# Decoder block on one core: token rows stored from ScalarE's queue, one gather ahead of a looped conditional part, and expert rows stored at once and added by eight adding gathers

## The chip, the cores and the metric

The kernel runs on one core of one Trainium2 chip. A core has a matrix engine (TensorE, here PE, with its weight loads as PEld), a vector engine (VectorE, DVE), an engine for activations and scaled copies (ScalarE, ACT), a general engine (GpSimd, POOL) and one that mostly issues transfers (SyncE, SP). Each engine runs its own instructions in their order; they wait for each other by semaphores. The metric is the device time of one execution in microseconds (us).

## The reference

One layer of a hybrid decoder, for 512 tokens of 1024 features in float32. The first half (a gated DeltaNet beside a gated MLP over the sequence) is untouched here. Its sum with the input is normalized per token; the result `h` goes into a mixture of 16 experts, and the sum of `h` and the experts' rows is normalized again:

```python
h = layer_norm(DEEPNORM_ALPHA * h + mix, ln1_g[l], ln1_b[l])
# routing: the best of 4 groups, in it the best 2 of 4 experts, with their weights
h_e = silu(t @ expert_w_gate[e]) * (t @ expert_w_up[e])      # 1024 -> 256
y  += combine[:, e] * (h_e @ expert_w_down[e])               # 256 -> 1024
h = layer_norm(DEEPNORM_ALPHA * h + ffn, ln2_g[l], ln2_b[l])
```

Every token goes to two experts.

## The kernel before

The 512 tokens are NT=4 tiles of 128 rows; `HT[:, i]` holds the rows of tile i (128 partitions by 1024 features). An instruction list in strings (L1015 to L1017) writes out the order of the first norm and the routing: `c`, `e` are parts of the last product of the first half, `t` transposes, `l` router logits, `f` is `finish(i)` (the norm of tile i), `g` is `choose(i)` (group and experts), `r` is `ranks(i)` (a token's place in its expert's list), and `w8` makes PE do eight products of no use.

`finish(i)` splits a row between engines: DVE does the first w columns (L965, L974), ACT and POOL the others (L971 to L973), with w=384, and 1024 for the last tile. It then stores the tile's rows in DRAM (`hD`, L975, from SP's queue).

`rank_tokens` (L1043) makes `idx`: for each expert a list of at most CAP=128 tokens. `gather(e)` (L1064) is a DMA that POOL issues: it fetches the rows of expert e's tokens from `hD` into one of five buffers `XG[e % 5]`. Two of them, gather(0) and gather(1), are issued ahead of a conditional part (L1100), which treats experts with more than 128 tokens in further blocks of 128; it is written out per block inside a loop over the experts. With these inputs no expert has as many, and every engine jumps over it, after it has read the largest count (L1097).

Weights come in 8 KB buffers (16 of them, per partition): `eload` (L800) loads a third of an expert (half of gate and up, or all of down), `esplit` (L818) splits it into a high part (ACT, L829) and a low part (DVE, L833), since each float32 product is done as three products of such parts (`kmm3`). A buffer that PE has used goes back to the ring and takes the next load (`release`, L1213); some are kept out of it.

For each expert `turn(e, hh)` (L1198) transposes its gathered rows on PE (L1205) and splits them on ACT (L1207) and DVE (L1208), `gate_up(e, part)` (L1226) does the first products in two halves, `swiglu` the gate, `down(e, n)` (L1242) the second product. `down` scales the result on ACT (L1261) into `yo[e]`. The experts are pipelined: in the loop's round e PE does `gate_up(e + 1)`, `turn(e + 2)` and `down(e)`.

What becomes of `yo[e]`: for e < E0=3 it is a gather buffer and is stored at once in DRAM (`yD`). For e = 3 to 11 (NL=12) it stays in SBUF, in buffers kept out of the ring of loads, and is stored after the last load of weights (L1359). Two rows of `yD` per token are then fetched by eight plain gathers (L1371) into `YG`, and added to `HT`: five adds by POOL (L1376), two by DVE at L1333, one by DVE at L1423. The rows of the last four experts are not stored: products with one-hot matrices (`rows_of_last`, L1272, PE L1278) place them. `total(i)` (L1384, DVE L1388) adds those to `HT`, and `inv_std`, `half1` (L1403) and `half2` do the second norm.

`K(...)` marks instructions that a scheduler leaves in the written order. The others, gathers among them, it may place elsewhere, as long as `tc.issue_after` and the data allow it.

## Time and profile before

| | us |
|---|---|
| time before, median of 3 runs | 812.68 (812.58 to 812.73) |
| profiled execution, its own time | 813.55 |
| its span in the trace | 811.8 |
| PE idle in 616.2 to 623.2 | 7.0 |
| one expert, from 641.4 to 650.8 on | 9.40 |
| last gather of `yD` rows issued | 776.5 |
| PE's last product ends | 792.2 |

The span is what the trace shows from the first to the last instruction; the execution's own time is 1.75 us more. A line of a timeline has the start, the time that a group took, the engine, the line of the code, and what it reads and writes. A number in square brackets is how long the engine had been idle, with what ended it.

### The profile page before, as it was taken

To read this page: it belongs to the slowest core of one execution; us is meant where nothing else is said; L and a number is where in the kernel's file an instruction comes from. 1 tells how busy PE (TensorE), PEld (TensorE's weight loads), DVE (VectorE), ACT (ScalarE), POOL (GpSimd) and SP (SyncE) were. 2 spreads that over 40 slices of the span, in tenths; PEclk is the share of its full clock that TensorE was granted. 3 is DMA by queue.
4 is the path that set the end of the run, shared out by engine and by line. 5 is a ranking of instruction groups with operands and counts; after the bars stand their busy time and mean duration, and the time that the engine had idled before them with its cause. 6 is when DMAs were issued, how large, how long until landed. Compare 5 with 4: busy or idle time off the path is not lost. (4 is left out here: it accounts for less than half of the span.)

```text
span 811.8 us, 10918 instructions
## 1 busy us (share of the span) xinstructions
PE 772.2 (95%) x4043; PEld 642.1 (79%) x4043; DVE 536.0 (66%) x1011; ACT 383.6 (47%) x646; POOL 114.7 (14%) x104
## 2 busy tenths in 40 slices
PE   8999999999999999999999999999985999999990
PEld 7688888887899988888888888888764788888780
DVE  3558954997567954357542322334598999999987
ACT  2545763553334624324222222222325999999833
POOL 2030002000100000002410101000132112100276
PEclk9999999999999999999999999999996999999996
DMA  9970045447230155234274323399628999999752
GB/s 232 225 210 16 1 74 135 80 99 150 52 89 2 29 128 103 63 95 104 44 200 122 92 84 91 100 326 343 212 96 274 345 381 382 368 346 289 275 227 103
DMA packets 105936, 133.65 MB, mean 165 GB/s; under 512 B 18628, under 2 KB 87672, under 8 KB 105880
## 3 DMA queue, kind: packets, MB, share of 16 engines
q1 hardware_dynamic: 101528, 118.08, 49.6%
q0 software_dynamic: 4352, 14.84, 5.4%
q8 instruction: 33, 0.54, 0.3%
q14 instruction: 23, 0.19, 0.1%
HBM read 120.82 MB, written 12.08 MB: 164 GB/s over the span
## 5 line engine op out<-in xcount | busy, mean ns | idle before, releaser
L239 PE MATMUL pa<-r,r 128*128 128x512 f32 (+1 forms) x688 | 268.8, 391 | 0.0
L240 PE MATMUL pa<-r,r 128*128 128x512 f32 (+1 forms) x688 | 268.2, 390 | 0.1
L241 PE MATMUL pa<-r,r 128*128 128x512 f32 (+1 forms) x688 | 267.8, 389 | 0.0
L150 DVE TENSOR_TENSOR r<-r,r 128x2048 fp32r<-128x2048 f32 (+2 forms) x57 | 103.6, 1821 | 126.5 <-ACT r L149 125.7
L149 ACT ACTIVATE r<-r 128x2048 fp32r<-128x2048 f32 (+2 forms) x57 | 86.7, 1528 | 137.3 <-PE pa L240 81.6
L239 PEld LDWEIGHTS pa<-r,r 128*128 128x128 f32 x688 | 129.4, 188 | 26.2 <-issue 0.9
L241 PEld LDWEIGHTS pa<-r,r 128*128 128x128 f32 x688 | 129.3, 188 | 25.7 <-DVE r L713 0.2
L240 PEld LDWEIGHTS pa<-r,r 128*128 128x128 f32 x688 | 129.3, 188 | 25.6 <-DVE r L745 0.5
L833 DVE TENSOR_TENSOR r<-r,r 128x1024 fp32r<-128x1024 f32 x96 | 117.1, 1222 | 4.7 <-ACT r L829 3.0
L829 ACT ACTIVATE r<-r 128x1024 fp32r<-128x1024 f32 x96 | 96.3, 1059 | 0.0
L1227 PE MATMUL pa<-r,r 128*128 128x512 f32 x192 | 78.1, 407 | 0.0
L1229 PE MATMUL pa<-r,r 128*128 128x512 f32 x192 | 75.9, 395 | 1.0 <-DVE r L1329 1.0
L1228 PE MATMUL pa<-r,r 128*128 128x512 f32 x192 | 75.6, 394 | 0.0
L398 DVE SCALAR_TENSOR_TENSOR r<-pa,r,r 128x509 f32<-128x509 f32 (+2 forms) x72 | 53.4, 746 | 9.9 <-ACT r L396 9.1
L1229 PEld LDWEIGHTS pa<-r,r 128*128 128x128 f32 x192 | 36.0, 188 | 9.8 <-DVE r L1329 1.9
L1228 PEld LDWEIGHTS pa<-r,r 128*128 128x128 f32 x192 | 36.3, 189 | 7.0
L1227 PEld LDWEIGHTS pa<-r,r 128*128 128x128 f32 x192 | 36.2, 189 | 7.1 <-ACT r L1207 0.2
L1066 POOL DMA_INDIRECT r<-hD,r x16 | 20.2, 1263 | 90.9 <-PE pb L1205 38.6
L399 ACT ACTIVATE r<-r 128x512 f32<-128x512 f32 x24 | 15.0, 627 | 31.9 <-DVE r L398 26.5
L782 POOL TENSOR_TENSOR r<-r,r 128x512 f32<-128x512 f32 x8 | 10.3, 1291 | 137.4 <-DVE r L781 133.2
L743 POOL TENSOR_TENSOR r<-r,r 128x512 f32<-128x512 f32 x8 | 14.2, 1787 | 98.0 <-DVE r L740 94.8
L396 ACT ACTIVATE r<-pa,r 128x512 f32<-128x512 f32 x24 | 16.3, 684 | 24.3 <-PE pa L241 24.3
(335 smaller groups left out, 934.5 us busy)
## 6 DMA issues: line engine op xcount, KB each, us to landing
r<-in_w_in_dram SPq DMA_DIRECT2D x22, 1024.0 KB, 8.4
r<-in_expert_w_gate_dram SPq DMA_DIRECT2D x32, 512.0 KB, 7.7
r<-in_expert_w_down_dram SPq DMA_DIRECT2D x16, 1024.0 KB, 8.9
r<-in_expert_w_up_dram SPq DMA_DIRECT2D x32, 512.0 KB, 8.1
r<-in_w_in_dram SPq DMA_DIRECT2D x20, 512.0 KB, 10.5
yD<-r SPq DMA_DIRECT2D x12, 512.0 KB, 9.7
r<-in_x_dram SPq DMA_DIRECT2D x8, 512.0 KB, 7.3
r<-in_w_dn_out_dram SPq DMA_DIRECT2D x4, 1024.0 KB, 5.2
```

Source lines behind the costliest of these rows:

```text
L149: pin(A.activation(hi, raw, AF.Copy))
L150: pin(eng.tensor_tensor(lo, raw, f_(hi), ALU.subtract))
L239: pin(T.matmul(o, lh, rh, start=first, stop=False))
L240: pin(T.matmul(o, lh, rl, start=False, stop=False))
L241: pin(T.matmul(o, ll, rh, start=False, stop=last))
L398: V.scalar_tensor_tensor(acc[:, s:], p[:, :S - s], wc(3 - s), acc[:, s:], op0=ALU.mult, op1=ALU.add)
L829: K(A.activation(hi[:, s], raw[:, s], AF.Copy))
L833: K(V.tensor_tensor(lo[:, s], raw[:, s], f_(hi[:, s]), ALU.subtract))
L1066: return G.indirect_dma_start(out=XG[e % 5], out_offset=None, in_=hD, in_offset=bass.IndirectOffsetOnAxis(ap=idx[:, e:e + 1], axis=0))
L1227: K(T.matmul(args[0], args[1], args[3], start=args[5], stop=False))
L1228: K(T.matmul(args[0], args[1], args[4], start=False, stop=False))
L1229: K(T.matmul(args[0], args[2], args[3], start=False, stop=args[6]))
```

## The change

Four things, in the order of the code.

1. `finish`: w=384 only for tiles 0 and 1, so tile 2 is DVE's alone, too. The store of the rows to `hD` is issued by ACT. The last `eload` is no longer held until the last such store. `w10` stands for `w8`, and 16 more products of no use follow the list.
2. Only gather(0) is issued ahead of the conditional part. Expert 0's first turns, a weight split and the first half of its products come ahead of it, too. Gathers 1 to 4 follow a fence (`gbehind`) behind it. The conditional part itself is now two loops, over blocks and over experts and blocks.
3. Every expert's rows, e < 12, are stored at once into `yD`, from ACT's queue, and `yo[e]` is always a gather buffer. Only one load buffer is kept out of the ring. gather(e + 5) is issued in round e.
4. In round 11, eight gathers with `compute_op=ALU.add` fetch rows of `yD` and add them to `HT[:, i]`. The plain gathers and the adds on POOL and DVE are gone.

```diff
     def finish(i):
-        w = 384 if i < NT - 1 else D
+        w = 384 if i < NT - 2 else D
...
-        stored[i] = SP.dma_start(hD[i * 128:(i + 1) * 128], HT[:, i])
+        A.dma_start(hD[i * 128:(i + 1) * 128], HT[:, i])
...
-                   t33 l33 f3 g3 w8 r3""".split():
+                   t33 l33 f3 g3 w10 r3""".split():
...
     eload()
-    with tc.issue_after(stored[NT - 1].ins):
-        eload()
+    eload()
...
     rank_tokens(idx, RO)
+    warm(16)
...
     earlier = esplit(0, True)
-    gather(0)
-    second = gather(1)
+    first = gather(0)
...
+    earlier()
+    turn(0, 0)
+    turn(0, 1)
+    esplit(1)
+    gate_up(0, 0)
...
-    with tc.issue_after(second.ins):
+    with tc.issue_after(first.ins):
         most = nc.values_load(cmi[0:1, 0:1], min_val=0, max_val=S,
...
-        for b in range(1, NBLK):
-            V.tensor_scalar(ork, rk2, float(CAP * b), None, op0=ALU.subtract)
+        V.tensor_copy(ork, rk2)
+        with tc.For_i(0, NBLK - 1, 1) as bo:
+            V.tensor_scalar(ork, ork, float(CAP), None, op0=ALU.subtract)
...
-            for b in range(1, NBLK):
-                SP.dma_start(oi, iD[bass.ds(eo * (NBLK - 1) + (b - 1), 1)].rearrange("b p o -> p (b o)"))
+            with tc.For_i(0, NBLK - 1, 1) as bo:
+                SP.dma_start(oi, iD[bass.ds(bo * NE + eo, 1)].rearrange("b p o -> p (b o)"))
...
+    gbehind = G.memset(gto[:, 1, 0:1], 0.0)
...
-    gather(2)
+    with tc.issue_after(gbehind.ins):
+        gather(1)
+        gather(2)
...
-    later()
-    turn(0, 0)
-    turn(0, 1)
     splits()
-    gate_up(0, 0)
-    gather(3)
-    gather(4)
+    gate_up(0, 1)
+    with tc.issue_after(gbehind.ins):
+        gather(3)
+        gather(4)
...
     def store(e):
-        SP.dma_start(yD[e * CAP:(e + 1) * CAP], yo[e])
+        K(A.dma_start(yD[e * CAP:(e + 1) * CAP], yo[e]))
...
-            yo[e] = reg(kept.popleft(), D) if e >= E0 else XG[(e + 2) % 5]
+            yo[e] = XG[(e + 2) % 5]
         K(A.activation(yo[e][:, ns], p, AF.Copy, scale=w_))
-        if n == 1 and e < E0:
+        if n == 1:
             store(e)
...
-        if E0 <= e < NL and (e == E0 or not (e - E0) % 2 == 0):
+        if e == E0:
             owed[0] += 1
...
-            for n in range(2):
-                K(V.tensor_tensor(HT[:, 0], HT[:, 0], YG[0][n], ALU.add))
...
-        if e <= E0:
-            gather(e + 5)
-        if e == E0:
-            gather(e + 6)
-        if e >= E0:
-            gather(e + 7)
+        gather(e + 5)
...
-        if e == NL:
-            with tc.issue_after(last_load[0].ins):
-                for m in range(E0, NL):
-                    store(m)
-        if e == NE - 3:
-            YG = [yo[m] for m in range(E0, NL)] + [reg(kept_rk, D)]
...
-            for i in range(NT):
-                for n in range(2):
-                    K(G.indirect_dma_start(out=YG[i][n], out_offset=None, in_=yD,
-                                           in_offset=bass.IndirectOffsetOnAxis(ap=sli[:, i, n:n + 1], axis=0)))
-            for i in range(1, NT):
-                for n in range(2):
-                    if i + n > 1:
-                        K(G.tensor_tensor(HT[:, i], HT[:, i], YG[i][n], ALU.add))
+        if e == NL - 1:
+            for n in range(2):
+                for i in range(NT):
+                    K(G.indirect_dma_start(out=HT[:, i], out_offset=None, in_=yD,
+                                           in_offset=bass.IndirectOffsetOnAxis(ap=sli[:, i, n:n + 1], axis=0),
+                                           compute_op=ALU.add))
...
-    K(V.tensor_tensor(HT[:, 1], HT[:, 1], YG[1][0], ALU.add))
```

What the change moves is seen in the order of each engine's instructions: line, operation, written<-read, shape, and the semaphores that it waits for (DMAHW and DMASW are those of transfers). The first piece is ACT at the start of the routing, as a difference; r_3260 is `HT`, L971 is in `finish`, L949 in `logits_part`, L938 in `transposes`.

```order
 L938 ACTIVATE r_4336<-pb 128x256 [waits PE_49,Activation_49]
 L971 ACTIVATE r_3260<-r_3260,r_3002,r_3000 128x640 [waits DVE_49]
+L975 DMA hD<-r_3260 128x1024 [waits DVE_49,DMAHW1_49,Activation_49,Pool_49]
 L949 ACTIVATE r_4312<-pa 20x128 [waits PE_49]
 L962 ACTIVATE r_4333<-r_2998,r_4331 128x1 [waits DVE_49]
-L938 ACTIVATE r_4337<-pb 128x256 [waits PE_49,Activation_49]
-L938 ACTIVATE r_4338<-pb 128x256 [waits PE_49,Activation_49]
+L938 ACTIVATE r_4337<-pb 128x256 [waits PE_49]
+L938 ACTIVATE r_4338<-pb 128x256 [waits PE_49]
 L971 ACTIVATE r_3260<-r_3260,r_3002,r_3000 128x640 [waits DVE_49]
-L949 ACTIVATE r_4312<-pa 20x128 [waits PE_49,Activation_49]
```

The store of a tile's rows now stands on ACT behind its L971, waiting for POOL and DVE, and ahead of the next L949.

The second place is POOL at the conditional part. Before, from the last step of `finish` on (r_4771 and r_4772 are the buffers of gathers 0 and 1):

```order
L973 TENSOR_TENSOR r_3260<-r_3260,r_4101 128x640 [waits Pool_49]
L1066 DMA r_4771<-hD,r_4741 128x1024 [waits DMAHW2_49,DMAHW4_49,DMAHW1_49,DMAHW7_49,DVE_49,Pool_49]
L1066 DMA r_4772<-hD,r_4741 128x1024
L1097 TENSOR_LOAD r_4769 [waits DVE_49]
L1100 COMPARE_AND_BRANCH
```

Both gathers stand ahead of the branch. At the end of the conditional part before (r_4773 is gather 2's buffer, the next into r_4771 is gather 5):

```order
L1100 UNCONDITIONAL_BRANCH
L1100 ISA [waits DMASW4_49,DMASW5_49,DMASW3_49,DMASW6_49,DMASW2_49,DMASW7_49,DMASW1_49,DMASW0_49]
L1100 UNCONDITIONAL_BRANCH
L1066 DMA r_4773<-hD,r_4741 128x1024 [waits DMASW4_49,DMASW5_49,DMASW3_49,DMASW6_49,DMASW2_49,DMASW7_49,DMASW1_49,DMAHW1_49,DMASW0_49,DMAHW4_49,DVE_49,DMAHW5_49,PE_49,Activation_49]
L1066 DMA r_4771<-hD,r_4741 128x1024 [waits PE_49]
```

The ISA row waits for all gathers issued so far. After, from the last step of `finish` on (r_4787 is expert 0's buffer; the second DMA into it is gather 5):

```order
L973 TENSOR_TENSOR r_3260<-r_3260,r_4101 128x640 [waits Pool_49]
L1066 DMA r_4787<-hD,r_4740 128x1024 [waits DMAHW2_49,DMAHW3_49,DMAHW1_49,DMAHW7_49,DVE_49,Pool_49]
L1066 DMA r_4787<-hD,r_4740 128x1024 [waits DMASW6_49,PE_49]
L1198 TENSOR_LOAD r_4785 [waits DVE_49]
L1201 COMPARE_AND_BRANCH
```

In gather 1's place stands gather 5. At the end of the conditional part after (r_4788 to r_4790 are the buffers of gathers 1 to 3):

```order
L1201 UNCONDITIONAL_BRANCH
L1201 ISA [waits DMASW4_49,DMASW5_49,DMASW3_49,DMASW6_49,DMASW2_49,DMASW7_49,DMASW1_49,DMASW0_49]
L1201 UNCONDITIONAL_BRANCH
L1263 MEMSET r_4871 128x1 [waits DVE_49]
L1066 DMA r_4788<-hD,r_4740 128x1024 [waits DMASW1_49]
L1066 DMA r_4789<-hD,r_4740 128x1024 [waits DMASW4_49,DMASW3_49,DMASW5_49,DMASW2_49,DMASW6_49,DMASW0_49,DMASW7_49,DVE_49,DMAHW1_49,PE_49,Activation_49]
L1066 DMA r_4790<-hD,r_4740 128x1024 [waits PE_49,Activation_49]
```

Gather 1 has moved from ahead of the branch to behind the fence (the MEMSET), and gather 5 from behind the conditional part to ahead of it, where it waits for a step of PE.

The third place is ACT in the round of expert 4. Before (r_5649 is the kept buffer of `yo[4]`):

```order
L1267 ACTIVATE r_5074<-pa 128x256 [waits DVE_49]
L829 ACTIVATE r_5637<-r_5301 128x1024 [waits DMAHW3_49]
L829 ACTIVATE r_5637<-r_5301 128x1024
L1261 ACTIVATE r_5649<-pa,r_4742 128x512 [waits PE_49] x2
L829 ACTIVATE r_5680<-r_5319 128x1024 [waits DMAHW5_49,DMAHW6_49,DVE_49,Activation_49]
L829 ACTIVATE r_5680<-r_5319 128x1024
```

Nothing stands between `down`'s steps and the next split copies. After (r_4788 is a gather buffer):

```order
L829 ACTIVATE r_5539<-r_5201 128x1024 [waits DMAHW3_49]
L829 ACTIVATE r_5539<-r_5201 128x1024
L1168 ACTIVATE r_4788<-pa,r_4741 128x512 [waits DMASW5_49,DMASW1_49,PE_49]
L1168 ACTIVATE r_4788<-pa,r_4741 128x512 [waits PE_49]
L1102 DMA yD<-r_4788 128x1024 [waits DMAHW3_49,Activation_49]
L829 ACTIVATE r_5581<-r_5219 128x1024 [waits DMAHW6_49,DVE_49]
L829 ACTIVATE r_5581<-r_5219 128x1024
```

The store of `yD` now follows the two steps of `down` on ACT, with a wait for a transfer's semaphore of its own, and the next split copies (L829) stand behind it.

## Rows read from the trace of the kernel before

**Rows 1.** The page of the profile: the span, and the line of each engine's busy time, its share of the span and its instructions.
```profile
span 811.8 us, 10918 instructions
...
PE 772.2 (95%) x4043; PEld 642.1 (79%) x4043; DVE 536.0 (66%) x1011; ACT 383.6 (47%) x646; POOL 114.7 (14%) x104
```

**Rows 2.** The table of stretches: from and to in us, length; then busy time and (in brackets) instructions of each engine, the clock granted to TensorE as a share of full speed, the DMA engines' mean busy share, and GB/s.
```profile
616.20:623.20 7.00, 0.00 (x0) 0.00 (x0) 5.55 (x25) 3.80 (x6) 2.08 (x2) 0.51 0.95 320
...
623.20:632.00 8.80, 8.76 (x45) 7.08 (x46) 7.78 (x18) 5.58 (x7) 4.28 (x4) 0.81 0.72 224
...
641.40:650.80 9.40, 9.40 (x48) 7.78 (x47) 9.30 (x11) 8.22 (x13) 0.00 (x0) 1.00 1.07 381
...
792.20:811.80 19.60, 0.00 (x0) 0.00 (x0) 14.12 (x34) 6.50 (x13) 12.31 (x10) 0.63 0.28 107
```

**Rows 3.** The timeline of VectorE in the routing: start us, us, engine, line, operation, out<-in, shape.
```profile
602.05 0.62 DVE L974 SCALAR_TENSOR_TENSOR r<-r,r,r 128x384 f32<-128x384 f32 x1
...
603.21 1.63 DVE L985 TENSOR_TENSOR r<-r 128x80 f32<-128x80 f32 x1
...
604.87 1.57 DVE L986 TENSOR_TENSOR r<-r,r 128x80 f32<-128x80 f32 x1
...
611.32 1.28 DVE L974 SCALAR_TENSOR_TENSOR r<-r,r,r 128x1024 f32<-128x1024 f32 x1
...
613.12 0.24 DVE L985 TENSOR_TENSOR r<-r 128x80 f32<-128x80 f32 x1
...
616.16 0.17 DVE L1050 CAST r<-pb 128x16 int32<-128x16 f32 x1
```

**Rows 4.** Around the first rows' store: a line of POOL's timeline, one of ACT's, and the instructions of line 975 on SyncE's queue in 612 to 613 us (durations ns min/median/max).
```profile
586.61 1.54 POOL L973 TENSOR_TENSOR r<-r,r 128x640 f32<-128x640 f32 x1
...
587.16 0.27 ACT L949 ACTIVATE r<-pa 20x128 f32<-20x128 f32 x1 [2.33 <-PE pa L947]
...
L975 SPq DMA_DIRECT2D hD<-r x1: 338/338/338, 612.6 to 612.6; - x1
```

**Rows 5.** POOL's timeline at the first gathers, and from the view of line 1066 how long a gather took from issue to landing, first for the one issued at 617.2, then for the one at 626.8.
```profile
617.15 1.11 POOL L1066 DMA_INDIRECT r<-hD,r  x1 [10.81 <-DVE r L1085]
...
626.81 0.94 POOL L1066 DMA_INDIRECT r<-hD,r  x1 [7.27 <-DVE r L1208]
...
DMA to landing us min/median/max: 5.9/5.9/5.9
...
DMA to landing us min/median/max: 4.7/4.7/4.7
```

**Rows 6.** PE's timeline from the pause on; in square brackets the idle time before a group and what ended it.
```profile
623.25 1.94 PE L1205 MATMUL pb<-r,r 128*128 128x128 f32 x8 [7.12 <-DVE r L1181]
...
625.02 0.79 PE L1227 MATMUL pa<-r,r 128*128 128x512 f32 x1
...
632.00 0.60 PE L1205 MATMUL pb<-r,r 128*128 128x128 f32 x4
...
632.46 0.48 PE L1227 MATMUL pa<-r,r 128*128 128x512 f32 x1
...
640.70 0.50 PE L1229 MATMUL pa<-r,r 128*128 128x512 f32 x1 [0.62 <-DVE r L1329]
```

**Rows 7.** The instructions of line 1100, the conditional part (q behind an engine's name is its sequencer): durations ns min/median/max, first and last start us.
```profile
L1100 PEldq COMPARE_BRANCH  x1: 5229/5229/5229, 616.7 to 616.7; - x1
...
L1100 DVEq COMPARE_BRANCH  x1: 76/76/76, 619.0 to 619.0; - x1
...
L1100 POOLq INC_SWDGE_SEM  x1: 512/512/512, 625.0 to 625.0; - x1
```

**Rows 8.** ACT's timeline in the twelfth and thirteenth expert.
```profile
746.48 1.27 ACT L1261 ACTIVATE r<-pa,r 128x512 f32<-128x512 f32 x2
...
753.22 0.60 ACT L1207 ACTIVATE r<-pb 128x512 fp32r<-128x512 f32 x1 [0.71 <-PE pb L1205]
```

**Rows 9.** The DMA view of 645 to 655 us (the mean rate, and the issues of the up weights: KB each, median us to landing), and the same issues in 685 to 695 us.
```profile
DMA packets 2632, 3.78 MB, mean 378 GB/s; under 512 B 98, under 2 KB 2247, under 8 KB 2632
...
r<-in_expert_w_up_dram SPq DMA_DIRECT2D x2, 512.0 KB, 8.1
...
r<-in_expert_w_up_dram SPq DMA_DIRECT2D x2, 512.0 KB, 10.8
```

**Rows 10.** The end of the kernel: line 1371's gathers and their landings, then lines of the timelines of POOL, DVE and PE.
```profile
L1371 POOL DMA_INDIRECT r<-yD,r x8: 937/956/1761, 765.4 to 776.5; - x8
...
DMA to landing us min/median/max: 5.3/10.1/10.6
...
781.44 13.86 POOL L1376 TENSOR_TENSOR r<-r,r 128x1024 f32<-128x1024 f32 x5 [4.04 <-DMA r<-yD,r]
...
777.40 2.47 DVE L1333 TENSOR_TENSOR r<-r,r 128x1024 f32<-128x1024 f32 x2
...
782.22 0.69 DVE L1388 SCALAR_TENSOR_TENSOR r<-pb,r 128x512 f32<-128x512 f32 x1 [0.36 <-PE pb L1278]
...
783.88 3.42 DVE L1423 TENSOR_TENSOR r<-r,r 128x1024 f32<-128x1024 f32 x1
...
799.92 0.68 DVE L1388 SCALAR_TENSOR_TENSOR r<-pa,r 128x512 f32<-128x512 f32 x1
...
790.18 1.98 PE L1278 MATMUL pb<-r,r 128*128 128x512 f32 x8
```

More of the change, by code (lines that the diff above doesn't have):

```diff
@@ L1189, in body @@
     FHL = carve(mixer_only, (2, 128), F32R)[0]
+    ZROW = NL * CAP
     yD = dram.tile([ZROW + 1, D], F32, name="yD")
@@ L1279, in rows_of_last @@
                            start=m == 0 and y is Y_LAST[m][0], stop=m == NE - NL - 1 and y is Y_LAST[m][1]))
+    earlier()
[3 more added lines that the diff above has]
+    gate_up(0, 0)
+    yO = dram.tile([(NBLK - 1) * NE * CAP, D], F32, name="yO")
+    iD = dram.tile([(NBLK - 1) * NE, CAP, 1], I32, name="iD")
+    with tc.issue_after(first.ins):
+        most = nc.values_load(cmi[0:1, 0:1], min_val=0, max_val=S,
+                              skip_runtime_bounds_check_because="a count of tokens")
@@ new lines, in body @@
+    A.activation(gto[:, 0, 0:1], ones[:, 0:1], AF.Silu)
+    SGB = cst(FF)
+    behind = V.memset(gto[:, 0, 1:2], 0.0)
+    gbehind = G.memset(gto[:, 1, 0:1], 0.0)
+    with tc.issue_after(behind.ins):
+        K(V.memset(SGB[0:4], 0.0))
+        GE, GB = cst(NT, 2, 16), cst(NT, 2, 3, 16, dt=BF16)
+        V.tensor_tensor(GE, EO, gt[:, :, :, None].to_broadcast([128, NT, 2, 16]), ALU.mult)
+        for n in range(3):
+            V.tensor_copy(GB[:, :, :, n], GE)
+            if n < 2:
+                V.tensor_tensor(GE, GE, GB[:, :, :, n], ALU.subtract)
+        slf, ovr = cst(NT, 2), cst(NT, 2)
+        V.tensor_scalar(ovr, rk2, float(CAP), None, op0=ALU.is_ge)
+        V.scalar_tensor_tensor(slf, eid, float(CAP), rk2, op0=ALU.mult, op1=ALU.add)
+        V.scalar_tensor_tensor(slf, ovr, float(ZROW), slf, op0=ALU.mult, op1=ALU.add)
+        V.tensor_scalar(sli, slf, float(ZROW), None, op0=ALU.min)
+        rs4 = cst(NT, NE - NL, 2)
+        V.tensor_tensor(rs4.rearrange("p i e n -> p i n e"), EO[:, :, :, NL:NE],
+                        rk2[:, :, :, None].to_broadcast([128, NT, 2, NE - NL]), ALU.mult)
+        V.tensor_reduce(rkv, rs4, axis=AX.X, op=ALU.add)
+        V.scalar_tensor_tensor(rkv, EA[:, :, NL:NE], -1.0, rkv, op0=ALU.add, op1=ALU.add)
@@ L1305, in body @@
     splits()
-    gate_up(0, 1)
     turn(1, 1)
```

151 lines of the change are left out of this document (59 added, 92 removed).

## Prediction

> **What bounds the kernel now.** I read the page's head first [rows 1]: TensorE (PE) is busy 772.2 of 811.8 us, so the question is where the other 39.6 lie. The table of stretches says it for this part of the kernel [rows 2]. From 616.2 to 623.2 PE does nothing: routing is done, the rows of expert 0 are being fetched. From 641.4 on each expert takes 9.40 us, all of them PE's; VectorE (DVE) has 9.30 of them and ScalarE (ACT) 8.22, and the DMA engines stand at a share of 1.07 with 381 GB/s. From 792.2 to the end PE is idle and DVE and GpSimd (POOL) finish the rows. So three stretches matter: the pause, the experts (bound by PE, with DVE and the DMA almost as full), and the tail. The timelines of each engine and the landings of the gathers give the waits inside them [rows 3 to 10].
>
> **Routing, up to the conditional part.** Two steps of the DVE chain, L985 and L986, take 1.63 and 1.57 us beside POOL's two steps of `finish(2)`, and 0.24 us each with POOL at rest [rows 3]. With i=2 all on DVE, POOL's part is gone: −1.63−1.57+2×0.24 = −2.7 us. DVE gets 1024 columns instead of 384 in its two steps; the row of i=3 has 1.28 for one against 0.62 for 384 columns: +1.3 us. Against it stands the stores' new queue. ACT is in order, and the store of rows 0 waits for POOL's last step, which ends at 586.61+1.54 = 588.15; L949, which ran at 587.16, stands behind it (the order's first place) and would start some 1.3 us later, with the 0.34 us of issuing that SP's store shows [rows 4]. PE had other work there, so I charge 0.5 of these 1.3; the same at `finish(1)` costs about as little. The cast of the list of indices goes ahead of another, −0.2. Sum −0.7 with 0.2 for the second store's wait; ends −1.6 (the stores cost nothing) and +1.0 (both cost 1.3 in full). The indices, written at 616.16+0.17 before, are there at about 615.6.
>
> **Gather 0 and the conditional part.** The first gather starts at 617.15 and lands 5.9 us after; a later one landed after 4.7 [rows 5]. Alone, and 0.7 earlier, I let gather 0 land at 616.45+4.5 = 621; turn 0 cost PE 1.94 us [rows 6] after a pause with a granted clock of 0.51 [rows 2], the 1.2 GHz level; I let it end at 622.5. The 16 extra warming products end before that and are in nobody's way. PE's jump over the skipped part took 5.23 us from 616.7 on, DVE's 0.08 [rows 7]. In the changed kernel the jump comes after turn 0 and five products. The skipped body shrinks on PE from 169 instructions to 75 by my count of the order's rows. If it still takes 5.2 us, PE is on at about 628 and its products end near 634; most of that lies under the wait below, but turn 1, which was done at 632.5 before, can't come sooner then. With a body half as long I give a cheap jump even odds.
>
> The Trainium skill ("Runtime: NRT & Kernel Launch", section "Instruction fetch mechanics") says that a taken branch whose target lies outside the two blocks at hand has to fetch it. That one jump of 5.23 us beside one of 0.08 agrees with it; whether 75 instructions are in reach no run here shows. By that rule a target in reach makes the jump cheap and leaves the first rival below open; by the row's 5.23 us it is closed, and the sum would be 1 more.
>
> **The second gather.** This is the part that costs. Before, gather 1 was issued ahead of the jump and had landed by 625.0, so that turn 1's second half ran at 632.00 straight behind PE's work [rows 6]. Now gather 1 stands behind the fence, and, by the order's second place, gather 5, which takes expert 0's buffer, has been moved ahead of the jump, where it waits for PE's turn 0. POOL's end of the conditional part (its ISA row, which is INC_SWDGE_SEM in the trace) waits until every gather issued so far has landed, as before: there it ran at 625.0 for 0.51 us, and the next gather came at 626.81, 1.8 after its start and 1.3 after its end [rows 5, 7]. Turn 0 ends at 622.5, gather 5 is out and lands 4.7 to 5.9 later, at 627.2 to 628.4; 1.3 to 1.8 us on, gather 1 starts at 628.5 to 630.2, and lands by 633.2 to 636.1. Meanwhile PE has turn 0 and the 24 products of expert 0, which took 625.02 to 632.0 before, some of it at half clock; now they end at about 629.5. It then waits some 5 us. Turn 1 (two times four transposes, 1.2 us by the 632.00 row, 1.94 at half clock) puts `gate_up(1,0)` at 634.5 to 638, and it was at 632.46: +2 to +5.6. The DVE splits that PE waited for at 640.70 (0.62) get done meanwhile, −0.6; the other gathers come in time. I take **+3.7 for routing and start together**, with +1 (the gathers land as fast as the 4.7 row) and +8 (the clock falls again and weights arrive later) as ends.
>
> **The experts.** PE keeps its 9.40 us each. Every store adds an issue on ACT; SP's same store took 0.34 us, and ACT has a gap of 0.71 us in front of L1207 in each expert [rows 8], so it hides; uncovered it would be 12×0.34 = 4 us. What I cannot hide so surely is its wait: each store waits for one of eight completion semaphores, whose earlier user is a weight load eight transfers back (the order's third place). Six transfers per expert of 9.40 us make eight 12.5 us on average; with the load that the order names I count 16. Queued behind it are the ACT copies from which DVE, and then PE, get the next weights. Loads landed after 8.1 us in 645 to 655 and after 10.8 in 685 to 695 [rows 9]. The stores of experts 3 to 11 now come there, 0.52 MB each, at about 378 GB/s 1.4 us more of DMA per expert. So landing grows from 8 by up to 1.4 per expert and touches 16 at the sixth: cost 0 if the DMA absorbs it, up to 6 us if the last four experts each take 1.4 more. I take +0.5.
>
> **The tail.** Eight plain gathers ran from 765.4 on, then five adds on POOL until 781.44+13.86 = 795.3, and three on DVE (1.24 each of two, and 3.42 beside POOL) [rows 10]. With all adds gone, `total(0)` is at 782.22 as before, but the last `total` no longer waits for 799.92. What is late next is PE, whose last L1278 ends at 790.18+1.98 = 792.16; DVE's `total(3)` can start at about 792.8. That is **−7.1**; the steps behind it keep their 12 us. Ends −5 (the products' rows wait for one another) and −7.7 (start at 792.2). The adding gathers start after expert 11's store, whose ACT step ran at 746.48 [rows 8]: its store lands at 754 to 756, then POOL issues eight in a row. No row shows an adding gather. Plain ones took POOL 0.94 to 1.76 us each and landed 5.3 to 10.6 us after [rows 10]; at that pace they end near 770, at double near 780, still ahead of 782.2. The bound below is the plain one; above, if each waits for the landing of the one before on its tile, two rounds of 10 us, also before 782.
>
> The Trainium skill ("Collectives: The Full Stack", "Why ReduceScatter is half of AllGather") says that an add inside a transfer needs two source reads, so that it moves half as much. By it the gathers would end near 780 rather than 770 and the sum would stay; but 2 us ahead of `total(0)` is little, and any further slowness would count in full, which speaks against this part of the change. No run here shows it.
>
> **Sum.** −0.7 and +4.4 (together the +3.7), +0.5, −7.1 = −2.9. The profiled execution took 813.55 us (its span is 811.8), so 810.65; it stood 0.87 above the median of 812.68, so I predict 809.8.
>
> **Rivals.**
> - *The start costs nothing* (+0 instead of +3.7): gather 5 and gather 1 land as the fast row does, and PE's weights for expert 1 are the wait. For it: 4.7 us landings; against it: the chain of two landings and 1.8 us is longer than PE's 7 us of work, and it needs the cheap jump. 806.
> - *The stall eats the gain*: the start costs 6 to 8, since the jump, the clock and the late splits add up. For it: the granted clock of 0.81 in 623.2 to 632 [rows 2] shows what a pause leaves behind. 812.7, no change.
> - *Slower, ScalarE held at its stores*: as soon as loads take longer to land than the eight transfers' lead, every expert lasts 11.0 instead of 9.40, what 4.19 MB (loads, gather, store) take at 381 GB/s. From the sixth expert to the tenth that is +8, so 817 with the forecast's other terms. For it: a DMA share of 1.07 [rows 2] and landings that grew [rows 9]; against it: they had come back to normal by the end, and the ring of load buffers gets four more.
> - *Slower, adding gathers drag*: if one costs more than 4 times a plain one, eight of them last past 795 and the tail is as long as before; +7 on the forecast, 817. Nothing here measures it.
>
> **Chances.** Forecast 0.42, its own range 806.5 to 811.8; free start 0.14; stall 0.17; ScalarE held 0.16; dragging gathers 0.11. A difference under 0.2%, 1.6 us, cannot be told from none, so no change means 811.1 to 814.3. Faster: 0.38 of the forecast, 0.14 and 0.01 of the stall make 0.53. No change: 0.04 of the forecast, 0.14 of the stall, and 0.03 of the last two, where their mechanism bites in part: 0.21. Slower: 0.24 from the last two and 0.02 from the stall, 0.26. The range 805 to 817 leaves out the far ends of the first and of the two slow cases, some 0.2 in all.
>
> **What would show it.** Right: a gap of PE of 4 to 6 us ahead of the transposes of expert 1, with gather 1 landing at its end; L985 of i=2 at 0.24; experts of 9.4 us; DVE's last `total` within 1 us of PE's last product. Wrong: no such gap, or one ahead of turn 0; ACT idle before its yD stores by more than 0.7 us with a load as releaser; HT's adds landing after 782, with `total` waiting on a DMA.

## The result and the profile after

The changed kernel takes 821.7 us (median of five runs, 820.5 to 826.3), the kernel before 812.73 beside it: a ratio of 1.0111, 95% interval 1.009 to 1.0133. It is slower by some 9 us; I had forecast 809.8 and a range up to 817.

The page after, the lines that answer to [rows 1]:

```profile
span 824.5 us, 10980 instructions
...
PE 784.0 (95%) x4079; PEld 650.7 (79%) x4079; DVE 525.2 (64%) x1008; ACT 381.7 (46%) x645; POOL 99.6 (12%) x98
```

The profiled execution, 826.25 us, was the longest of the five. Its span is 12.7 us longer than that of the kernel before, and 3.9 of them lie ahead of everything that was changed: PE waited 2.65 us ahead of L507 at 142.2 behind a late load of `w_in`, and the granted clock in the 3.8 us behind it was 0.55. So I compare lengths of stages, not times on the clock. The table has them for every kernel of this study, read from PE's timelines: from the first router transpose (L935) to the last product of `rank_tokens`, from there to turn 0 (the transposes of expert 0), on to the turn of expert 4, to that of expert 15, to the end of PE's last product, and to the end.

| us | ahead | routing | to turn 0 | to turn 4 | to turn 15 | to PE's end | to the end | span |
|---|---|---|---|---|---|---|---|---|
| before | 573.7 | 42.3 | 7.3 | 32.2 | 103.3 | 33.4 | 19.7 | 811.8 |
| changed | 577.5 | 43.2 | 8.3 | 40.2 | 109.1 | 33.7 | 12.4 | 824.5 |
| e1_fence5 | 573.5 | 43.7 | 8.5 | 38.0 | 109.4 | 33.7 | 12.4 | 819.1 |
| e2_hold | 572.1 | 43.1 | 7.3 | 40.4 | 109.1 | 33.7 | 12.4 | 818.2 |
| e3_ydpool | 573.9 | 43.7 | 8.6 | 39.0 | 104.9 | 34.1 | 13.4 | 817.5 |
| e4_hdsp | 573.5 | 41.9 | 5.8 | 40.6 | 108.9 | 33.6 | 12.4 | 816.9 |
| e5_tail_act | 572.8 | 42.4 | 7.0 | 33.0 | 110.5 | 33.9 | 12.4 | 812.0 |
| e6_tail_pool | 574.6 | 42.4 | 7.1 | 33.1 | 108.7 | 32.7 | 13.4 | 812.0 |
| e7_undo3 | 572.4 | 41.9 | 5.7 | 35.8 | 110.9 | 32.6 | 13.4 | 812.6 |
| e8_loop | 572.5 | 42.3 | 7.2 | 32.6 | 103.1 | 33.3 | 19.2 | 810.3 |
| e9_tail_sp | 575.5 | 42.3 | 7.4 | 33.3 | 103.3 | 34.1 | 12.4 | 808.3 |
| e10_tail_sp_w | 572.8 | 40.9 | 6.5 | 34.9 | 103.3 | 34.1 | 12.4 | 804.9 |
| e11_undo_sp | 572.6 | 41.1 | 5.9 | 36.8 | 103.3 | 33.2 | 12.4 | 805.4 |
| e12_split_first | 572.5 | 41.0 | 6.3 | 36.2 | 103.7 | 34.0 | 12.4 | 806.1 |

By this table the change wins 7.3 us in the tail and loses 9.9 at the start (0.9, 1.0 and 8.0) and 5.8 in the experts; with 0.3 elsewhere that is +8.7, and the medians say +9.0. There is one profile of each kernel: e1 and e3 change nothing in the routing, and it takes 43.7 in them for 43.2 in the changed kernel, so half a microsecond in one column proves nothing.

**The start.** PE's timeline after, the lines that answer to [rows 6], and one from the routing (L949 is `logits_part`'s copy on ACT):

```profile
592.78 0.63 PE L947 MATMUL pa<-r,r 128*20 128x128 f32 x8 [1.76 <-ACT r L949]
...
629.06 1.97 PE L1112 MATMUL pb<-r,r 128*128 128x128 f32 x8 [4.47 <-DMA r<-hD,r]
...
642.18 1.94 PE L1112 MATMUL pb<-r,r 128*128 128x128 f32 x8 [3.65 <-DMA r<-hD,r]
...
644.01 0.79 PE L1134 MATMUL pa<-r,r 128*128 128x512 f32 x1
```

PE waits 1.76 us for L949, 4.47 for the rows of gather 0, and 3.65 for those of gather 1.

The end of the routing hides one more cost. First a line of the kernel before, where PE waits for DVE's L993 ahead of the last ranks; then two of the changed kernel, the products of no use (L228; `w10` stands as 20 in the trace, `w8` as 16) and DVE behind them:

```profile
614.82 0.17 PE L1001 MATMUL pb<-r,r 128*128 128x16 bf16 x1 [1.33 <-DVE r L993]
...
615.04 4.64 PE L228 MATMUL pb<-r 128*128 128x128 f32 x20
...
619.82 0.17 DVE L1003 SCALAR_TENSOR_TENSOR r<-r,pb 128x16 f32<-128x16 f32 x1 [1.07 <-PE pb L1001]
```

Now DVE waits 1.07 us for PE, which is still at products of no use. The indices come later by that much.

POOL after, answering to [rows 5]:

```profile
624.60 1.24 POOL L1066 DMA_INDIRECT r<-hD,r  x1 [22.89 <-SPq L1201]
...
631.31 0.98 POOL L1066 DMA_INDIRECT r<-hD,r  x1 [5.47 <-PE pb L1112]
...
636.38 0.10 POOL L1263 MEMSET r<- 128x1 f32 x1 [4.09 <-DMA r<-hD,r]
...
637.06 0.98 POOL L1066 DMA_INDIRECT r<-hD,r  x1 [0.57 <-issue]
```

The list of indices was written at 621.1, but gather 0 starts at 624.60. What it waited for is the last row store, on ACT's queue now (its issue and its landing; the last line is its landing in the kernel before, where it was issued at 612.6):

```profile
L975 ACTq DMA_DIRECT2D hD<-r x1: 326/326/326, 616.3 to 616.3; - x1
...
DMA to landing us min/median/max: 7.4/7.4/7.4
...
DMA to landing us min/median/max: 3.2/3.2/3.2
```

It lands at 623.7, behind five loads that SP had issued from 610.5 to 612.6. Gather 5 starts at 631.31, as soon as turn 0 is done, and lands 4.4 us later; only then does POOL leave the conditional part, and gather 1 starts at 637.06. This is the chain that I had worked out. The jump itself, [rows 7], is cheap now:

```profile
L1201 PEldq COMPARE_BRANCH  x1: 228/228/228, 632.1 to 632.1; - x1
```

**The experts.** The table of stretches after, columns as in [rows 2]:

```profile
640.00:650.00 10.00, 7.06 (x24) 5.39 (x25) 4.94 (x7) 6.64 (x10) 2.58 (x3) 0.66 0.92 347
...
670.00:680.00 10.00, 10.00 (x50) 8.29 (x49) 9.53 (x11) 9.17 (x15) 0.94 (x1) 1.00 1.07 380
...
740.00:750.00 10.00, 8.62 (x43) 6.79 (x43) 9.03 (x10) 7.42 (x12) 0.94 (x1) 1.00 1.06 384
...
780.00:790.00 10.00, 9.16 (x43) 7.18 (x42) 9.90 (x13) 6.46 (x10) 6.72 (x5) 1.00 1.02 192
```

In 670 to 680 PE is full. From 721 on it waits once in each of four experts, 0.6 us in the first and some 1.4 in the others; from one turn to the next it is then 10.2 us and three times 11.05, where it was 9.4. The second of these waits:

```profile
732.14 0.50 PE L1136 MATMUL pa<-r,r 128*128 128x512 f32 x1 [1.42 <-DVE r L1333]
```

ACT's timeline there, which answers to [rows 8] (ACTq is ACT's sequencer, which issues the store), and the view of one weight load's line, issued at 702.6:

```profile
713.36 1.27 ACT L1168 ACTIVATE r<-pa,r 128x512 f32<-128x512 f32 x2
...
715.74 0.33 ACTq L1102 DMA_DIRECT2D yD<-r  x1
...
716.17 2.01 ACT L829 ACTIVATE r<-r 128x1024 fp32r<-128x1024 f32 x2 [1.54 <-DMA r<-in_expert_w_up_dram]
...
L812 SPq DMA_DIRECT2D r<-in_expert_w_up_dram x1: 1372/1372/1372, 702.6 to 702.6; - x1
...
DMA to landing us min/median/max: 13.1/13.1/13.1
```

ACT has finished `down` at 714.63 and issues the store at 715.74: it stands there for 1.1 us, and for 2.2 in the next three experts. The load that it waits for was issued at 702.58 and landed 13.1 later, at 715.7. It is the one eight transfers back, with the same semaphore. From its issue to the end of `down` there were 12.05 us. For the four stores before it that stretch was 13.5 to 13.9 us, and the loads concerned had landed after 7.6, 8.2, 10.3 and 13.0: they reached the store's lead, and at the seventh expert they passed it. The split copies behind the store come late, then DVE's, then PE's products. Their own data were not late: those split at 727.2, behind the next store, had landed at 717.2.

**The tail.** The adding gathers, which stand in the place of [rows 10]; the queue of the gathers in 780 to 790, with plain gathers in 766 to 778 of the kernel before below it (packets, MB, share of the DMA engines' time); and DVE's first and last `total`:

```profile
L1359 POOL DMA_INDIRECT r<-yD,r x8: 1538/1666/2276, 773.0 to 789.3; - x8
...
DMA to landing us min/median/max: 6.9/9.9/13.7
...
q0 software_dynamic: 528, 1.92, 101.9%
...
q0 software_dynamic: 519, 1.92, 47.5%
...
802.19 0.69 DVE L1373 SCALAR_TENSOR_TENSOR r<-pb,r 128x512 f32<-128x512 f32 x1 [0.34 <-PE pb L1185]
...
812.61 0.68 DVE L1373 SCALAR_TENSOR_TENSOR r<-pa,r 128x512 f32<-128x512 f32 x1
```

From the first issue at 773.0 to the last landing at 803.0 they take 30 us. `total(0)` starts at 802.19 and waits for PE alone, since the last gathers are those of the last tiles; the last `total` starts at 812.61, 0.5 us after PE's last product, where it had been 7.8 us after it.

### The profile page after: what moved, and what is told of

Its sections match the earlier page's. It is cut to its first block, busy times and chain, and to the rows that moved or that the text cites. A ratio compares the mean times of both kernels' runs of the same rounds, so it can differ in the third digit from the quotient of the medians.

```text
span 824.5 us, 10980 instructions
## 1 busy us (share of the span) xinstructions
PE 784.0 (95%) x4079; PEld 650.7 (79%) x4079; DVE 525.2 (64%) x1008; ACT 381.7 (46%) x645; POOL 99.6 (12%) x98
## 5 line engine op out<-in xcount | busy, mean ns | idle before, releaser
L829 ACT ACTIVATE r<-r 128x1024 fp32r<-128x1024 f32 x96 | 96.3, 1057 | 14.8 <-DMA r<-in_expert_w_up_dram 9.8
L1136 PE MATMUL pa<-r,r 128*128 128x512 f32 x192 | 77.0, 401 | 6.0 <-DVE r L1333 5.9
L1134 PE MATMUL pa<-r,r 128*128 128x512 f32 x192 | 79.4, 414 | 0.0
L1135 PE MATMUL pa<-r,r 128*128 128x512 f32 x192 | 76.5, 399 | 0.0
L1066 POOL DMA_INDIRECT r<-hD,r x16 | 17.6, 1100 | 123.6 <-ACT r L1168 39.8
L399 ACT ACTIVATE r<-r 128x512 f32<-128x512 f32 x24 | 15.0, 627 | 33.4 <-DVE r L398 28.1
L1112 PE MATMUL pb<-r,r 128*128 128x128 f32 x128 | 20.7, 292 | 8.2 <-DMA r<-hD,r 8.1
L1114 ACT ACTIVATE r<-pb 128x512 fp32r<-128x512 f32 x32 | 19.0, 594 | 19.4 <-PE pb L1112 19.3
L1115 DVE TENSOR_TENSOR r<-pb,r 128x512 fp32r<-128x512 f32 x32 | 21.9, 683 | 9.2 <-ACT r L1114 9.2
## 6 DMA issues: line engine op xcount, KB each, us to landing
r<-in_expert_w_up_dram SPq DMA_DIRECT2D x32, 512.0 KB, 10.1
```

What stands on the lines that cost most here:

```text
L829: K(A.activation(hi[:, s], raw[:, s], AF.Copy))
L1115: K(V.tensor_tensor(XGL[:, hs], v3(p), f_(XGH[:, hs]), ALU.subtract))
L1134: K(T.matmul(args[0], args[1], args[3], start=args[5], stop=False))
L1135: K(T.matmul(args[0], args[1], args[4], start=False, stop=False))
L1136: K(T.matmul(args[0], args[2], args[3], start=False, stop=args[6]))
```

## The experiments

Times are medians; beside each stands the ratio to the kernel before on the same chip, with its 95% interval. The kernel before took 814.0, 813.6 and 813.2 us in the three sets. Ratios of the changed kernel (1.0111) come from another set, so small differences to it are read from the table of stages.

**e1_fence5: gather 5 alone behind the fence.**

```diff
-        gather(e + 5)
+        if e == 0:
+            with tc.issue_after(gbehind.ins):
+                gather(5)
+        else:
+            gather(e + 5)
```

> Gather 5 alone is put behind the fence, as gathers 1 to 4 are; nothing else changes. Theory: gather 1 started at 637.06 in the changed kernel because the conditional part's end waited for gather 5 (issued at 631.31, landed at 635.7). Without it the end waits for gather 0 alone, gather 1 starts some 5 to 6 us sooner (about 2 us after turn 0 began), lands before PE has finished expert 0, the wait of 3.65 us ahead of turn 1 goes, and with it the half clock behind it: 4 to 5.5 us less than the changed kernel's 821.3, so 816 to 817.5. Rival: gather 1 is late for another reason (the jump, the fence's own wait for DVE, the loads), then gather 1 still starts more than 10 us after gather 0 and the time stays 820.5 to 822.

820.47 us, 1.0075 (1.006 to 1.009). POOL and PE:

```profile
628.99 1.14 POOL L1066 DMA_INDIRECT r<-hD,r  x1 [0.16 <-issue]
...
636.00 1.06 PE L1112 MATMUL pb<-r,r 128*128 128x128 f32 x8 [1.13 <-issue]
...
642.81 0.41 PE L1331 MATMUL pb<-r,r 128*128 128x128 f32 x2 [2.13 <-DVE r L1175]
```

Gather 1 starts 3.4 us after turn 0 began (8.0 before this edit), and the wait ahead of turn 1 falls from 3.65 to 1.13. So gather 5 did hold gather 1. But from turn 0 to turn 4 only 2.2 us come back: a wait of 2.13 for DVE's L1175 (0.73 before this edit) takes most of the place of the one removed. The theory has the cause right and the gain too large.

**e2_hold: the last row store on SP, the last loads behind it.**

```diff
-        A.dma_start(hD[i * 128:(i + 1) * 128], HT[:, i])
+        stored[i] = (SP if i == NT - 1 else A).dma_start(hD[i * 128:(i + 1) * 128], HT[:, i])
...
-    eload()
-    eload()
+    with tc.issue_after(stored[NT - 1].ins):
+        eload()
+        eload()
```

> Only the last tile's row store goes back to SP's queue, and the last loads of weights stand behind it there, as before. Theory: gather 0 started 3.5 us after the list of indices was written because the last row store, issued behind five loads, took 7.4 us to land. With the loads behind it the store lands in 3 to 4 us, gather 0 starts at most 0.6 us after the list, everything behind moves up by 2.5 to 3.3 us: 818 to 819. Rival: gather 0 waits for POOL or for the indices: no change, 820.5 to 822.

820.44 us, 1.0087 (1.0071 to 1.0103). POOL, and the landing of this gather:

```profile
616.50 1.16 POOL L1067 DMA_INDIRECT r<-hD,r  x1 [20.21 <-DVE r L1084]
...
DMA to landing us min/median/max: 6.0/6.0/6.0
```

Gather 0 starts 1.4 us after the last product of `rank_tokens` began, where it had been 4.0: the store was its wait. But its landing grows from 4.4 to 6.0, and turn 0 comes only 1.0 us sooner. SP issued three loads from 611.3 to 612.7, behind the store; I take them for the cause, as before the change, where two such loads went ahead of a landing of 5.9. The theory named the wait and missed that the transfer which no longer waits meets the same loads.

**e3_ydpool: the stores of expert rows on POOL.**

```diff
-        K(A.dma_start(yD[e * CAP:(e + 1) * CAP], yo[e]))
+        K(G.dma_start(yD[e * CAP:(e + 1) * CAP], yo[e]))
```

> The stores of expert rows are issued by POOL instead of ACT; their number, time and bytes stay. Theory: from the sixth expert on ACT stood 1.5 to 2.6 us at its store, whose semaphore was that of a load that landed 13 us after its issue, and DVE and PE starved behind it. Off ACT, the gaps of PE of 1.4 us in four experts go: 4 to 5 us less than 821.3, so 816 to 817.5. Rival: the DMA engines' rate sets the pace, stores and loads together are more than they can move in 9.4 us; then the experts keep lasting 11.05 us with ACT waiting for loads instead, 820.5 to 822.

820.44 us, 1.0085 (1.0069 to 1.0102). The stretch from 740 on:

```profile
740.00:750.00 10.00, 10.00 (x52) 8.30 (x51) 9.38 (x12) 9.24 (x14) 1.58 (x2) 1.00 1.06 383
```

PE is full at the same 383 GB/s at which it had lost 1.4 of 10 us. So the rate of the DMA engines alone does not stop PE, and the rival falls as it was stated. It does set the pace of the stores: POOL issues them some 11 us apart now (697.1, 708.4, 719.1, 730.5), while an expert takes 9.4; e9 comes back to this. The 5.8 us shrink to 1.6, which lie in the last of these experts, ahead of turn 15. The tail is 1 us longer. The gain in time is smaller than stated, for the reason that e6 shows.

**e4_hdsp: all row stores of the first norm back on SP.**

```diff
-        A.dma_start(hD[i * 128:(i + 1) * 128], HT[:, i])
+        SP.dma_start(hD[i * 128:(i + 1) * 128], HT[:, i])
```

> All four row stores of the first norm go back to SP's queue, the scheduler puts the last one ahead of the last load. Theory: the same gain as with the last store alone (2 to 3 us, a little less since three loads stay ahead of it), and 1 us more since L949 on ACT no longer waits 1.4 us twice for POOL's part: 817 to 818.5. Rival: ACT's waits at the stores are hidden behind PE's other products: then the same as with the last store alone, 818 to 819.5.

817.33 us, 1.0044 (1.003 to 1.0059).

```profile
587.36 0.63 PE L947 MATMUL pa<-r,r 128*20 128x128 f32 x8 [0.35 <-ACT r L949]
...
621.30 1.76 PE L1112 MATMUL pb<-r,r 128*128 128x128 f32 x8 [1.99 <-DMA r<-hD,r]
```

PE's wait for L949 is 0.35 again (1.76 in the changed kernel). The routing falls by 1.3 us to 41.9, which is 0.4 less than before the change, and turn 0 follows after 5.8 instead of 8.3. The time is in the range of the theory. ACT's waits at the stores were not hidden: the rival falls.

**e5_tail_act and e6_tail_pool: the kernel before with only the end of the change.** The edit to the kernel before, in e5; e6 has `G` in the place of `A`. The plain gathers of the tail, their adds and the kept buffers go, as in the change.

```diff
-        SP.dma_start(yD[e * CAP:(e + 1) * CAP], yo[e])
+        K(A.dma_start(yD[e * CAP:(e + 1) * CAP], yo[e]))
...
-            yo[e] = reg(kept.popleft(), D) if e >= E0 else XG[(e + 2) % 5]
+            yo[e] = XG[(e + 2) % 5]
...
+        if e == NL - 1:
+            for n in range(2):
+                for i in range(NT):
+                    K(G.indirect_dma_start(out=HT[:, i], out_offset=None, in_=yD,
+                                           in_offset=bass.IndirectOffsetOnAxis(ap=sli[:, i, n:n + 1], axis=0),
+                                           compute_op=ALU.add))
```

> The kernel before with only the end of the change: every expert's rows stored at once from ACT, five gather buffers, eight adding gathers, no adds on POOL and DVE. Theory (the tail gives 7.2, ACT's wait at its stores takes 5.5 to 7 back): 0.5 to 2 us less than the kernel before, with PE gaps of about 1.4 us in three to five experts and 12.4 us from PE's last product to the end (19.7 before). Rival: the loss in the experts came from the late start of the changed kernel, whose loads stood still in the pause; then no gaps, and 7 us less than before.

> As the last one, but with the stores issued by POOL. Theory: no gaps in the experts up to the fourteenth, a gap of 1 to 2 us late, where the adding gathers and one-hot steps wait for the last stores, tail 12.4 to 13.4: 4 to 6 us less than the kernel before. Rival (the DMA engines are the bound with nine more stores in the stream): within 1 us of the kernel before.

e5: 813.7 us, 1.0006 (0.9992 to 1.0019). One of its gaps:

```profile
741.55 0.50 PE L1229 MATMUL pa<-r,r 128*128 128x512 f32 x1 [1.37 <-DVE r L1329]
```

The tail is 12.4 us here, too, and the stretch from turn 4 to turn 15 has 7.2 more: what the adding gathers win, ACT's stores give back, with nothing changed at the start. The theory's own figure of 5.5 to 7 for that loss was a little low, so none of its 0.5 to 2 us is left. The rival, that the gaps come from the late start, falls.

e6: 813.56 us, 1.0009 (0.9993 to 1.0025), not the 4 to 6 less of the theory but the time of the rival. POOL, DVE and PE:

```profile
721.80 2.00 POOL L1066 DMA_INDIRECT r<-hD,r  x1 [9.31 <-issue]
...
732.97 1.71 POOL L1066 DMA_INDIRECT r<-hD,r  x1 [8.59 <-PE pb L1205]
...
755.68 0.49 DVE L1350 TENSOR_SCALAR r<-r,r 128x512 fp32r<-128x512 bf16 x1 [4.54 <-DMA yD<-r]
...
758.96 0.77 PE L1229 MATMUL pa<-r,r 128*128 128x512 f32 x1 [3.58 <-DVE r L1329]
```

POOL's gathers, with a store behind each, are 11 us apart, longer than an expert, so its stores fall behind. In the round of the twelfth expert DVE stands 4.54 us at its first one-hot matrix, which is written over a gather buffer whose store has not landed, and PE waits 3.58 behind it. The experts run at 9.4 us until then; the bill comes at once. So the rival has a part in it, the stores do fall behind, though no expert before the twelfth is held by it.

**e7_undo3: the changed kernel with gather 5 behind the fence, row stores on SP, and expert rows on POOL.** (The edits of e1, e4 and e3 together.)

> The changed kernel with three parts undone at once: row stores on SP, gather 5 behind the fence, expert rows stored by POOL. Theory: the three gains, 3.8 and 2.2 and 2.6 to 5 us in the traces, are of separate places and add up: 821.3 less 8.6 to 11, 810.5 to 812.7, with 18.8 us for two experts up to the fourteenth and 36 to 38 us from turn 0 to the fourth expert's turn (32.3 before, 40.2 in the changed kernel). Rival: they share a cause (the DMA load at the start), then less than 6 us come back, 815 or more.

814.95 us, 1.0025 (1.001 to 1.0041), above what was expected. The table shows the gains of the start together (routing 41.9, to turn 0 5.7, to turn 4 35.8), and in the experts a loss as large as ever: POOL's late stores again, as in e6, in one wait of 5.1 us of PE at 759. I had added up the gains without this wait. The time lies just under the rival's 815, but a shared cause at the start is not what the table shows.

**e8_loop: the kernel before with the looped conditional part alone.** (The loop over experts; the one over blocks goes the same way.)

```diff
...
-            for b in range(1, NBLK):
+            with tc.For_i(0, NBLK - 1, 1) as bo:
...
```

> The kernel before with only the conditional part as loops, which is jumped over. Theory: PE's jump falls from 5.23 us to under 0.5, but turn 0 waits for gather 0, which landed at 623.05, so turn 0 starts as before and the time stays within 1 us. Rival: PE was held by the jump too, then turn 0 starts earlier and the time falls by 1 us or more.

814.28 us, 1.0015 (1.0005 to 1.0025).

```profile
L1100 PEldq COMPARE_BRANCH  x1: 352/352/352, 615.6 to 615.6; - x1
```

The jump costs 0.35 us for 5.23, and the time does not fall: turn 0 comes 7.2 us after the routing, as before (7.3). The 5 us had been cover for gather 0's landing.

**e9_tail_sp and e10_tail_sp_w: the end of the change with stores on SP, without and with tile 2 on DVE.** e9 is e5 with `SP.dma_start` in `store`. e10 adds:

```diff
-        w = 384 if i < NT - 1 else D
+        w = 384 if i < NT - 2 else D
```

> The kernel before with only the end of the change, the stores of expert rows issued by SP (as it did for the first three). Theory: SP has no work of PE's path behind it but loads that run some 13 us ahead, so the wait for a semaphore costs nothing; no gaps in the experts, 12.4 us behind PE's last product: 5 to 7.2 us less than the kernel before. Rival 1: loads behind a waiting store come so late that splits starve as on ACT: 0 to 2 us less. Rival 2: as with POOL, the one-hot steps wait on late stores at the fourteenth expert: 0 to 3 us less.

> The last one with tile 2's norm all on DVE, too. Theory: the routing takes 0.4 us less (41.9 for 42.3 in the trace with stores back on SP), so 0 to 0.5 less than the last one. Rival: two loads that the scheduler now puts ahead of the last row store delay gather 0: 1 to 2 us more than the last one.

e9: 807.17 us, 0.9924 (0.9911 to 0.9937). Its stretch from 740 on:

```profile
740.00:750.00 10.00, 10.00 (x51) 8.25 (x50) 9.63 (x12) 9.26 (x14) 1.66 (x1) 1.00 1.07 378
```

PE is full, at 1.07 of the DMA engines and 378 GB/s. From turn 4 to turn 15 it takes 103.3 us, as before the change, and the tail 12.4. The gain is within the theory's 5 to 7.2 us, and both rivals fall.

Why does SP's wait cost nothing? Two of SP's stores, and then the table of stretches for one expert and for the last one ahead of turn 15, first in the changed kernel, then here:

```profile
709.62 1.91 SPq L1195 DMA_DIRECT2D yD<-r  x1
...
720.54 1.99 SPq L1195 DMA_DIRECT2D yD<-r  x1
...
737.56:748.61 11.05, 9.68 (x49) 7.69 (x47) 9.04 (x11) 8.47 (x12) 0.94 (x1) 1.00 1.06 383
...
769.05:778.44 9.39, 9.39 (x49) 7.76 (x48) 9.29 (x12) 9.02 (x13) 4.88 (x3) 1.00 0.40 76
...
724.32:733.70 9.38, 9.38 (x49) 7.76 (x48) 9.01 (x11) 8.64 (x13) 1.83 (x1) 1.00 1.06 389
...
752.48:761.88 9.40, 9.40 (x48) 7.75 (x47) 8.67 (x12) 8.63 (x13) 0.61 (x1) 1.00 0.64 261
```

SP's stores are 11 us apart as well. They come 1.8 us after `down` for the fifth expert and 7.3 after it for the eighth. In the changed kernel an expert that ACT holds moves 383 GB/s times 11.05 us, 4.2 MB, which is what the prediction counts for an expert with its store (4.19). Here one moves 389 times 9.38, 3.65 MB; the rest is put off to the stretch ahead of turn 15, which has time to spare (261 GB/s for 76). From turn 4 to turn 15 the bytes are the same, 38.6 and 38.8 MB. So the DMA engines are behind in both kernels: from ACT's queue that stops PE at once, from SP's it is made up later. Little was left: DVE's first one-hot matrix waits 0.63 us for a store here, 4.54 in e6. More experts with stores were not tried.

e10: 805.17 us, 0.9905 (0.9893 to 0.9918): 8 us less than the kernel before and the fastest of the study. The routing takes 40.9, 1.4 less than before, where I had expected 0.4. The traces have the reason: the 0.4 came from e4, which has `w10`, and this kernel has `w8`:

```profile
608.79 3.78 PE L228 MATMUL pb<-r 128*128 128x128 f32 x16
```

In both kernels DVE's last L993 starts 39.4 us after the first router transpose; the last L1001, which needs it, starts at 40.8 in e4 behind 20 products (4.64 us) and at 39.7 here. From turn 0 to turn 4 it takes 1.6 us more than e9, so by the table it gains 0.8 on e9, where the medians say 2.0.

**e11_undo_sp and e12_split_first: the changed kernel with stores on SP.** e11 has gather 5 behind the fence and both kinds of stores on SP. e12 adds:

```diff
     earlier()
+    esplit(1)
     turn(0, 0)
     turn(0, 1)
-    esplit(1)
     gate_up(0, 0)
```

> The changed kernel with both kinds of stores on SP and gather 5 behind the fence. Theory: the start loses 3.5 us from turn 0 to the fourth expert's turn and wins 1.5 ahead of it, the experts lose nothing, the tail wins 7.2: 4 to 6 us less than the kernel before, 808 to 810. Rival: SP's waiting stores hold the loads as ACT held the splits: 812 or more.

> The last one with the second weight split written ahead of expert 0's turns. Theory: in the changed start ACT idled 4.9 us behind PE's turn 0 with split copies queued after it, and PE paid 2.15 us later for a late step of DVE. With the copies in the idle time the split is done before the turn, and 1 to 2.2 us of the 3.5 come back: 1 to 2 us less than the last one. Rival: the copies delay turn 0's own step on ACT, or the 2.15 us have another cause: within 0.5 us of the last one.

e11: 808.61 us, 0.995 (0.9936 to 0.9964), as the theory has it: three parts taken back from the change turn +1.1% into −0.5%. From turn 0 to turn 4 it is still 4.6 us longer than the kernel before.

e12: 809.57 us, 0.9961 (0.9948 to 0.9974): no gain. PE and ACT:

```profile
636.23 0.41 PE L1331 MATMUL pb<-r,r 128*128 128x128 f32 x2 [2.12 <-DVE r L1175]
...
630.15 0.60 ACT L1114 ACTIVATE r<-pb 128x512 fp32r<-128x512 f32 x1 [4.83 <-PE pb L1112]
...
630.64 2.00 ACT L829 ACTIVATE r<-r 128x1024 fp32r<-128x1024 f32 x2
...
632.54 0.59 ACT L1114 ACTIVATE r<-pb 128x512 fp32r<-128x512 f32 x1
```

The wait of 2.1 us for L1175 is there as before. So the split queued behind turn 0 is not its cause; the theory falls. The rows suggest another: both halves of turn 1 come at once now, and a split copy of 2.0 us stands between their two steps on ACT (630.15 and 632.54). That was not tried and stays open.

## Why the prediction was wrong

Two steps failed: that the last row store would land in time for gather 0, and that the stores of expert rows would wait for nothing on ACT. A third, the routing, was wrong by less.

- **Routing, −0.7: wrong.** It was +0.9. (The term's own parts, −2.7, +1.3, −0.2, +0.5 and +0.2, add up to −0.9.) DVE's part was right: L985 and L986 ran free of POOL as worked out, and with the stores on SP (e10) DVE's last L993 comes 1.6 us sooner than before, as −2.7+1.3−0.2 says. ACT's wait at its first store, of which I charged 0.5 us because "PE had other work there", is a wait of PE (1.76 us for 0.36) and costs 1.4. The last 1.1 us are `w10`, to which I gave no price: its products end after DVE has what the last ranks need. In the changed kernel gather 0 waits still longer for the store, so these 1.1 do not show in the time.
- **Gather 0 at 616.45: wrong.** It landed in 4.4 us, as taken (4.5), but started 3.5 us after the list of indices. That the last load no longer stood behind the last row store was in the change, and I gave it no price; the store's landing went from 3.2 to 7.4 us. Turn 0 came 51.5 us after the first router transpose; my 621 is 47.3, and the 4.2 between them are as much as the landing grew. e2 and e4 show the wait.
- **The jump: right**, 0.23 us, at even odds, and worth nothing by itself (e8). The rule of the Trainium skill ("Runtime: NRT & Kernel Launch", "Instruction fetch mechanics") fits: 75 skipped instructions cost 0.23 and 169 cost 5.23, both by the prediction's count. The queues of instructions moved three packets in 616.5 to 622.2 of the kernel before, during the long jump, and none in 631.9 to 632.6 of the changed one.
- **The second gather: the mechanism right, its size as well.** From turn 0 to `gate_up(1,0)` I had 13.5 to 17 us; it was 14.95. The +4.4 became +9.0 because turn 0 itself came 1.9 us later than before instead of some 2 sooner, and because eight of the 12 products behind the wait ran at the half clock (3.6 us for 1.9). The 0.6 that I took off for DVE's splits was not there: waits of 0.73 and 0.30 stand in place of 0.62. With 9.9 for routing and start the sum lies beyond my upper end of 8.
- **The experts, +0.5: wrong.** It was +5.8, by the mechanism that I had written down: the store waits for the semaphore of the load eight transfers back, with the split copies queued behind it. I had two numbers for the lead, 12.5 us from the average and 16 from my count, and took the larger; it was 13.5, then 12.05 at the seventh expert, and the loads landed after 13.1. The rival's price of 11.0 us per expert, from the DMA engines' rate, was right: 11.05. ACT, once it waits for loads, goes at the pace at which 4.2 MB are moved. Where the rival has five slow experts, four were, the first of them by half.
- **The tail, −7.1: right**, −7.3. By what the Trainium skill says of inline adds ("Collectives: The Full Stack", "Why ReduceScatter is half of AllGather"; it says it of ReduceScatter) the adding gathers would move at half rate, and the trace agrees: in 780 to 790 the DMA engines are as busy (1.02) as in 740 to 750 (1.06) and move 192 GB/s instead of 384. Beside plain gathers, 1.92 MB cost 101.9% of 10 us for 47.5% of 12, 1.8 times as much. It cost nothing, since 803.0, 0.8 us after `total(0)` began, was still ahead of what needs the last of them.
- The sign was lost in the sum: routing, start and experts were each taken below the middle of their bounds. The rival of ScalarE held at its stores was right in kind and place, but I gave it 0.16 and let it stand alone; with the start's +9.9 in place of +3.7 the two together are the result. Two of the signs that I had named for being wrong are there: a gap of PE ahead of turn 0 (4.47 us), and ACT idle ahead of its stores for more than 0.7 us behind a load.

## What to carry to other kernels

A DMA issued from a compute engine's queue can stop that engine: it waits for its data, for the semaphore that it shares with an earlier transfer, and everything behind it waits along. Before moving a store there, compare the landing of the transfer that used the semaphore last with the time between the two, and put it on the queue that has nothing urgent behind it. Count, too, what a round of the loop has to move: here it was 4.2 MB, 11 us at the rate of the DMA engines, for 9.4 us of PE's work. Then something falls behind, and the queue of the store decides whether that is the engine on which all wait. Where a transfer is freed from an order (a load behind a store), ask what it now runs ahead of.
